# A decoder layer in split float32: buffers of the raw and the low weight parts, and the order of the low products

## The chip, the cores and the metric

The kernel runs on one core of one Trainium2 chip. The metric is the device time of one execution in microseconds (us); lower is better. The core has five engines that each work through a queue of their own, in order: TensorE (PE, with its weight loads shown apart as PEld), VectorE (DVE), ScalarE (ACT), GpSimd (POOL) and SyncE (SP, which here issues the DMAs). [...]

## The reference, cut to what matters

One pre-norm decoder layer over 1024 tokens of width 1024, in float32:

```python
h = rms_norm(x, attn_norm)
z = h @ w_in
a_conv, q, kc_r, vc_r, ks, vs, kw, vw, g = jnp.split(z, splits, axis=-1)
conv_out = conv_mixer(a_conv, ...)              # GLU, causal conv of width 31, LayerNorm, silu
kc = compress(kc_r, cmp_k_pe, cmp_k_w1, cmp_k_w2)
vc = compress(vc_r, cmp_v_pe, cmp_v_w1, cmp_v_w2)
nsa_out = nsa_attention(q, kc, vc, ks, vs, kw, vw, gates)
x = x + concatenate([conv_out, nsa_out]) @ w_out
h = rms_norm(x, ffn_norm)
gate, up = split(h @ w_gate_up)
x = x + (silu(gate) * up) @ w_down
return rms_norm(x, final_norm)
```

The attention has 12 query heads over 4 groups of keys and values and three gated branches: compressed blocks, eight selected blocks, and a window of 512 tokens.

## The kernel before

**Products in split float32.** A product of two float32 matrices is made of three products of parts: each operand is split into a high part (a rounded copy) and a low part (what the copy lacks), and high times high, high times low and low times high are summed in one PSUM bank. The product of the two low parts is left out.

**Weights.** `load_w` (L214) brings one chunk of weights: 128 partitions with up to 1096 numbers each, 512 KB for a chunk of 128 columns. Its steps, in order: one or two DMAs by SP into a raw tile (L224), a cast by ACT into the high tile (L225), and a subtraction by POOL, in four pieces, into the low tile (L229; for the first two chunks it is one piece on DVE). The tile pool `wp` has two raw buffers, three high ones and three low ones. A raw buffer is free again when the low part has been made; a high or low buffer when the last product with it is done. While the first half of the attention runs (`phase[0] == 0`), L220 puts a one-column copy by POOL ahead of the load, which reads a row sum of the attention four steps back (`PACE_B = 4`), so that the load can't start before it.

**Feeds.** A `Feed` (L193) holds a list of such loads. Taking chunk n (`get`) issues the loads up to chunk n+2; a taker that holds two chunks at a time takes the second with `get(1)`, which issues one less.

**Who uses chunks, in order.** Ahead of the attention the feed `first` gives: four chunks for the convolution's input (`conv_in`, each one `gemm_t`: 8 contraction steps with 3 products, 24 products of 512 columns), two for the keys to be compressed (`compress_in`, each used for both halves of the tokens, in the order half 0 with chunks 0 and 1, then half 1 with chunks 0 and 1), two for the window values (`values`, four tiles of tokens in `value_tile`, 24 products of 274 columns each, both chunks in every tile), then four chunks of the compression's first weight in turn with four query chunks (`compress`, 24 products of 264 columns a chunk; `project_d`), two more query chunks, and the same again for the compressed values with four key chunks. Two value chunks at the very start are used tile by tile while the tokens arrive. In all that is chunks 0 to 29.

**The attention** (`attention`, L697) works on 128 queries and one group at a time, first for tokens 0 to 511, then 512 to 1023. `weave` (L175) lays products of a second stream, `fill`, between its products: in the first half `fill_b` (L971), the projections of the second half of the tokens (chunks 30 to 47, by the same helpers), and then, in `fill_all` (L1404), the first output projection (`out_proj`, chunks of `w_out` through another feed) and the feed-forward part. Per step of the attention: products of queries and keys (L788, L792), a fused add with row minimum on DVE (L796), exp on ACT (L799), row sums and their reciprocals on DVE (L803, L804), a scaling on POOL (L809), transposes on PE (L815), the split of the transposed tile by ACT and DVE (L233), and products with the values (L832, L833). `cmp_stage` (L616) makes the compressed branch: products L628, adds on DVE (L630, L632), exp on ACT (L642), scalings on POOL (L646, L650), transposes (L656) and their split (L661, L662), and a store (L663).

**What sets the order.** The program is built with `TileContext(nc, schedule_with_timeline_sim=True)`: a list schedule takes, at each point of a model of the timeline, the first instruction in program order that is ready, and so fixes each engine's queue. On the chip the queues run in that order whatever the real durations are. `Drive` (L149) ties side streams to the matmul that they are emitted behind.

In the functions below the order of the three products is the same everywhere: for each contraction step high with high, then the weights' low part, then the activations' low part:

```python
for a, b in ((wh, hhi), (wl, hhi), (wh, hlo)):
```

Of the kernel before, what the change touches and what calls it, by code (L numbers as in the profile page):

```python
# [12 lines left out]
F32 = mybir.dt.float32  # L13
F32R = mybir.dt.float32r
# [5 lines left out]
P = 128  # L20
# [3 lines left out]
KT = DM // P  # L24
# [24 lines left out]
WCH = 1096  # L49
# [39 lines left out]
def tile_hymba(ctx: ExitStack, tc, x, attn_norm, w_in, conv_w, conv_b, conv_ln_g, conv_ln_b,  # L89
# [10 lines left out]
    wp = ctx.enter_context(tc.tile_pool(name="weights", bufs=3, side="left"))  # L100
# [5 lines left out]
    def bank(name, tag="z"):  # L106
        return ps.tile([P, 512], F32, tag=tag, name=name, bufs=BANKS[tag])
# [27 lines left out]
    MM = 0.216  # L135
# [8 lines left out]
    def mm(*args, **kw):  # L144
        lastpe[0] = pe.matmul(*args, **kw)  # L145
# [62 lines left out]
    def acc_bank(name):  # L208
        turn[0] += 1
        return bank(name, turn[1][turn[0] % len(turn[1])])  # L210

    pace = []

    def load_w(parts, a, b, eng=pool):  # L214
        raw = wp.tile([P, WCH], F32, tag="raw", name="w_raw", bufs=2)
        hi = wp.tile([P, WCH], F32R, tag="whi", name="w_hi")
        lo = wp.tile([P, WCH], F32R, tag="wlo", name="w_lo")
        back = PACE_B if phase[0] == 0 else PACE_C
        if len(pace) >= back > 0:
            pool.tensor_copy(raw[:, 0:1], pace[-back][:, 0:1])  # L220
        n = a * b
        v = raw[:, :n].rearrange("p (k c) -> p k c", k=a)
        for c, src in parts:
            sp.dma_start(v[:, :, c:c + src.shape[-1]], src.rearrange("(k p) c -> p k c", p=P))  # L224
        act.copy(hi[:, :n], raw[:, :n])  # L225
        step = n // PIECES if eng is pool else n
        for c in range(0, n, step):
            q = slice(c, c + step)
            eng.tensor_sub(lo[:, q], raw[:, q], hi[:, q].bitcast(F32))  # L229
        return (hi[:, :n].rearrange("p (k c) -> p k c", k=a), lo[:, :n].rearrange("p (k c) -> p k c", k=a))  # L230

    def split(hi, lo, src):
        return act.copy(hi, src), dve.tensor_sub(lo, src, hi.bitcast(F32))  # L233
# [34 lines left out]
    def quarters(h, w):  # L268
        if h:
            return [pm.tile([P, 4, 512], F32R, tag=("act", "x1")[w], name="h1", bufs=2) for _ in range(2)]  # L270
        return [pa.tile([P, 4, 512], F32R, name=f"h0_{w}_{j}") for j in range(2)]

    hhi = [quarters(h, 0) for h in range(2)]
    hlo = [quarters(h, 1) for h in range(2)]

    def win_chunk(c0):
        return load_w([(0, w_in[0, :, c0:c0 + P])], KT, P)
# [7 lines left out]
    def value_tile(ws, g0, dst, t):  # L285
        hf = t // 4
        o = acc_bank("vo")
        n = 0
        tt = slice((t % 4) * P, (t % 4 + 1) * P)
        for k in range(KT):  # L290
            wh, wl = ws[k // 4]
            for a, b in ((hhi, wh), (hhi, wl), (hlo, wh)):
                mm(o[:, :274], a[hf][k // 4][:, k % 4, tt], b[:, k % 4, :], start=n == 0, stop=n == 3 * KT - 1)
                n += 1
                yield 0.117
        vv = p1.tile([P, GROUPS, 2, HD], F32R, tag="vv", name="vv", bufs=2)
        split(vv[:, :, 0, :], vv[:, :, 1, :], o[:, :256].rearrange("p (g d) -> p g d", g=GROUPS))
        dve.tensor_copy(gates[:, t, g0:g0 + 18], o[:, 256:274])
        sp.dma_start(dst[t * P:(t + 1) * P, :, :], vv.bitcast(F32).rearrange("p g s d -> p g (s d)"))
# [14 lines left out]
    for t in range(6):  # L314
# [7 lines left out]
        if t == 0:  # L322
# [5 lines left out]
            for j, copy in enumerate((dve.tensor_copy, act.copy)):  # L328
                b = bank("gb", "s")
# [87 lines left out]
        pool.tensor_copy(base[:, T + P:], base[:, 512:768])  # L417

    def gemm_t(o, wh, wl, hf):
        n = 0  # L420
        for k in range(KT):
            for a, b in ((wh, hhi), (wl, hhi), (wh, hlo)):
                mm(o, a[:, k, :], b[hf][k // 4][:, k % 4, :], start=n == 0, stop=n == 3 * KT - 1)
                n += 1
                yield MM

    def project_d(feed, dst, row, halves, scaled=False):
        wh, wl = feed.get()
# [37 lines left out]
    def silu(u, th):  # L466
        act.activation(th, u, AF.Tanh)
        dve.scalar_tensor_tensor(u, th, 1.0, u, op0=ALU.add, op1=ALU.mult)

    def compress(xh, xl, feed, w2, tag, out):  # L470
        hs = [bank("h0", tag), bank("h1", tag)]
        n = 0
        for jc in range(4):
            wh, wl = feed.get()
            if jc == 1:
                w2r = pa.tile([P, 2, HD], F32, tag="w2r", name="w2r")
                pool.tensor_copy(w2r[:, 0, 0:1], wh[:, 0, 0:1].bitcast(F32))
            for j4 in range(4):
                j, s = (jc * 4 + j4) % 8, jc // 2
                for a, b in ((wh, xh), (wl, xh), (wh, xl)):  # L480
                    for ht in range(2):
                        mm(hs[ht][:, :264], a[:, j4, ht * P:(ht + 1) * P], b[:, j, :, s:s + 66],
                           start=n < 2, stop=n >= 94)
                        n += 1
                        yield 0.12
        ah = pa.tile([P, 2, 256], F32R, tag="ah", name="ah")
        al = pa.tile([P, 2, 256], F32R, tag="al", name="al")
        for ht in range(2):
            bc = pa.tile([P, 1], F32, tag="bc", name="bc", bufs=2)
            dve.tensor_scalar(bc, hs[ht][:, 64:65], 0.5, None, op0=ALU.mult)  # L490
            af, th = [pa.tile([P, 256], F32, tag="af", name="af", bufs=2) for _ in range(2)]
            dve.tensor_scalar(af.rearrange("p (g n) -> p g n", g=GROUPS),
                              hs[ht][:, :264].rearrange("p (g n) -> p g n", g=GROUPS)[:, :, 0:64],
                              0.5, bc, op0=ALU.mult, op1=ALU.add)
            silu(af, th)
            split(ah[:, ht, :], al[:, ht, :], af)
        sp.dma_start(w2r, w2[0].rearrange("(t p) d -> p t d", p=P))
        w2h = pa.tile([P, 2, P], F32R, tag="w2h", name="w2h")
        w2l = pa.tile([P, 2, P], F32R, tag="w2l", name="w2l")
        for c in range(2):  # L500
            split(w2h[:, :, c * HD:(c + 1) * HD], w2l[:, :, c * HD:(c + 1) * HD], w2r)
        out.extend((ah, al, w2h, w2l))
# [389 lines left out]
    def q_load(m):  # L892
        return lambda: win_chunk(C_Q + m * P)

    def kv_loads():
        return [lambda c=c, m=m: win_chunk(c + m * P) for m in range(2) for c in (C_KW, C_KS)]
# [74 lines left out]
    def fill_b():  # L971
        f1 = Feed([q_load(0), q_load(1)] + value_loads(C_VS, 0) + [q_load(2)] + value_loads(C_VW, 18)
                  + [q_load(m) for m in (3, 4, 5)] + kv_loads() + conv_loads())
        for m in (0, 1):
            yield from project_d(f1, q_d, m * P, (1,), True)
        yield from values(f1, 0, vs_d, 1)
        done.add(("q", 0))
        yield from project_d(f1, q_d, 2 * P, (1,), True)
        done.add(("q", 1))
        yield from values(f1, 18, vw_d, 1)  # L980
        done.update({("v", 0), ("v", 1)})
        for m in (3, 4):
            yield from project_d(f1, q_d, m * P, (1,), True)
        done.add(("q", 2))
        yield from project_d(f1, q_d, 5 * P, (1,), True)
        done.add(("q", 3))
        for dst in (kw_d, ks_d):
            yield from project_d(f1, dst, 0, (1,))
        done.add(("kv", 0))
        for dst in (kw_d, ks_d):  # L990
            yield from project_d(f1, dst, P, (1,))
        done.add(("kv", 1))
        yield from conv_in(f1, 1)
        done.add(("conv", "in"))
# [19 lines left out]
    for (g, qt), at in zip(stages, CMP_AT):  # L1014
        s = cmp_stage(g, qt)
# [47 lines left out]
    def mixed(si, kq):  # L1063
        return ("conv", si) in done and all(("mix", g, i) in done for g in range((2, GROUPS)[kq]) for i in SETS[si])
# [338 lines left out]

    def fill_all():  # L1404
        yield from fill_b()
        while not mixed(0, 0):
            yield -1.0
        mix = mix_in(0, 0, pm)
        set_in(0, pm)
        x_in(0, 0)  # L1410
        x_in(0, 1)
        yield LEAD_C
        yield from out_proj(feed, 0, "z", mix, 0)

        while not mixed(0, 1):
            yield -1.0
        p1_stack.close()
        last["p3"], p = open_pool("p3", "left")
        mix2 = mix_in(0, 1, p, "h21")
        yield from out_proj(feed, 0, "z", mix, 1)  # L1420
        yield MIXLAT
        for ch in range(2):
            yield from out_proj(feed, 0, "z", mix2, ch)
        set_norm(0, p)
        yield from ffn_norm_in(0, "z")
        for _ in range(NF // 2):
            yield from ffn(feed, (0,), FT)
# [87 lines left out]
```

## Time and profile before

| | us |
|---|---|
| three runs | 1472.18, 1472.75, 1474.23 |
| median | 1472.75 |
| profiled execution | 1470.28 |
| its span | 1468.6 |
| its granted TensorE clock | 0.995 |
| PE busy | 1422.3 |
| PEld busy | 1228.5 |
| DVE busy | 1035.2 |
| ACT busy | 771.9 |
| POOL busy | 693.0 |

Times in views are microseconds from the span's start. A row of a timeline gives the start, the duration, the engine, the line, the operation, out<-in with its form, and the count of equal instructions merged; in brackets stands the engine's idle time just before and what ended it. The ends of matmuls are modelled, so that PE appears busy across short pauses; a pause is better seen between the weight loads, as each matmul has one. SPq is the queue of SP, where a row is the issue of a DMA. DMA rows in the chain run from the issue to the landing.

### The profile page before, as it was taken

How to read it: one execution, taken by the hardware profiler on the slowest of the kernel's cores; microseconds unless marked ns; L12 is line 12 of the kernel's file. 1: busy time of each engine (PE TensorE's matmuls, PEld its weight loads, DVE VectorE, ACT ScalarE, POOL GpSimd, SP SyncE). 2: the span in 40 equal slices, each digit the busy share in tenths (PEclk: the TensorE clock that was granted, in tenths of full speed). 3: DMA queues.
4: the chain of work that ended last, by engine and by line, in shares of the span. 5: the costliest groups of instructions: out<-in, count | busy, mean ns of one | idle time of the engine just before them, and what ended most of it. 6: DMA issues, size and time to landing. Idle time of an engine off the chain costs nothing.

```text
span 1468.6 us, 23484 instructions
## 1 busy us (share of the span) xinstructions
PE 1422.3 (97%) x7995; PEld 1228.5 (84%) x7995; DVE 1035.2 (70%) x2279; ACT 771.9 (53%) x1602; POOL 693.0 (47%) x972
## 2 busy tenths in 40 slices
PE   7999999998999999999999999999999999999997
PEld 6888888886878788888888888777887899999996
DVE  5893486778776667687577785512538988788885
ACT  6333466768665566756657564312425544444443
POOL 4666584767665455655655556644568000000001
PEclk9999999999999999999999999999999999999999
DMA  6336578757597244345245213744234433323321
GB/s 218 89 96 187 150 221 243 194 181 214 140 288 218 78 106 121 92 106 132 85 101 137 76 48 98 212 133 150 80 105 155 142 101 107 95 87 115 111 62 72
DMA packets 234246, 196.34 MB, mean 134 GB/s; under 512 B 14745, under 2 KB 204029, under 8 KB 234126
## 3 DMA queue, kind: packets, MB, share of 16 engines
q1 hardware_dynamic: 234126, 194.84, 45.8%
q8 instruction: 63, 1.03, 0.3%
q14 instruction: 57, 0.47, 0.1%
HBM read 161.04 MB, written 33.75 MB: 133 GB/s over the span
## 4 chain that ended last, share of the span: by engine, by line
PE 73%; DVE 10%; DMA 7%; POOL 4%; ACT 3%; issue 2%; SPq 1%; ACTq 0%; POOLq 0%; DVEq 0%
PE gu L1154 17%; PE dn L1173 14%; PE yy L1301 7%; PE pt L815 5%; PE zo L145 4%; PE zz L1301 3%; PE wo L1088 3%; DMA w_raw<-in_w_in_dram 3%; PE s L788 3%; PE o L833 3%; PE o L832 3%; DVE cacc L571 2%; POOL w_lo L229 2%; PE vo L145 2%; DMA o_raw<-in_w_out_dram 2%
## 5 line engine op out<-in xcount | busy, mean ns | idle before, releaser
L229 POOL TENSOR_TENSOR w_lo<-w_raw,w_hi 128x256 fp32r<-128x256 f32 (+1 forms) x504 | 406.0, 837 | 161.0 <-ACT w_hi L225 154.1
L1154 PE MATMUL gu<-h,w_hi 128*128 128x512 f32 x768 | 253.0, 398 | 0.6 <-DVE x L1178 0.6
L1173 PE MATMUL dn<-w_hi,aw 128*128 128x512 f32 x656 | 230.7, 397 | 1.6 <-DVE x L1178 1.2
L225 ACT CAST w_hi<-w_raw 128x1024 fp32r<-128x1024 f32 (+1 forms) x147 | 152.7, 1051 | 130.6 <-DMA w_raw<-in_w_in_dram 43.1
L809 POOL TENSOR_SCALAR pr<-pr,l,gates 128x640 f32<-128x640 f32 (+5 forms) x192 | 148.4, 785 | 122.4 <-DVE l L804 96.0
L233 DVE TENSOR_TENSOR pl<-pt,ph 128x384 fp32r<-128x384 f32 x264 | 140.4, 551 | 54.8 <-ACT ph L233 52.8
L799 ACT ACTIVATE pr<-pr,m 128x640 f32<-128x640 f32 (+5 forms) x192 | 141.5, 737 | 71.0 <-DVE m L796 69.2
L1154 PEld LDWEIGHTS gu<-h,w_hi 128*128 128x128 f32 x768 | 143.2, 188 | 29.5 <-DVE x L1178 1.0
L233 ACT CAST ph<-pt 128x384 fp32r<-128x384 f32 x264 | 118.9, 478 | 81.2 <-PE pt L815 61.6
L1383 POOL TENSOR_TENSOR rs<-rs,mhalf 128x1 f32<-128x1 f32 x4 | 2.6, 643 | 319.1 <-DVE rs L1382 318.9
L1154 PE MATMUL gu<-h,w_lo 128*128 128x512 f32 x384 | 152.3, 397 | 0.0
L1173 PEld LDWEIGHTS dn<-w_hi,aw 128*128 128x128 f32 x656 | 123.2, 188 | 27.5 <-DVE x L1178 2.1
L1178 DVE TENSOR_TENSOR x<-dn,x 128x512 f32<-128x512 f32 x168 | 113.4, 685 | 42.2 <-PE dn L1173 41.5
L815 PE MATMUL pt<-ident,pr 128*128 128x128 f32 x792 | 136.8, 273 | 5.0 <-DVE pl L233 3.7
L1173 PE MATMUL dn<-w_lo,aw 128*128 128x512 f32 x328 | 129.6, 395 | 0.0
L796 DVE CUSTOM_DVE_ANT_0 pr<-s,base 128x384 f32<-128x384 f32 (+3 forms) x192 | 101.2, 533 | 33.2 <-PE s L792 19.8
L815 PEld LDWEIGHTS pt<-ident,pr 128*128 128x128 f32 x792 | 101.4, 140 | 22.5 <-issue 3.2
L145 PE MATMUL zo<-h,w_hi 128*128 128x512 f32 x320 | 106.9, 402 | 2.0 <-ACT w_hi L225 1.2
L1247 ACT CAST w_s<-sum 128x512 fp32r<-128x512 f32 x80 | 49.3, 621 | 106.8 <-PE yy L1301 89.5
L788 PE MATMUL s<-kt,q 128*128 128x384 f32 (+3 forms) x288 | 100.8, 352 | 4.3 <-DVE m L796 1.8
L832 PE MATMUL o<-ph,vt 128*128 128x384 f32 x264 | 98.7, 374 | 2.3 <-ACT ph L233 1.3
L1301 PEld LDWEIGHTS yy<-term,w_s 128*128 128x128 f32 x720 | 93.1, 188 | 8.4 <-DVE c L1316 3.5
(271 smaller groups left out, 3163.7 us busy)
## 6 DMA issues: line engine op xcount, KB each, us to landing
w_raw<-in_w_gate_up_dram SPq DMA_DIRECT2D x48, 512.0 KB, 3.9
w_raw<-in_w_down_dram SPq DMA_DIRECT2D x43, 512.0 KB, 3.6
w_raw<-in_w_in_dram SPq DMA_DIRECT2D x40, 512.0 KB, 4.3
u_raw<-in_w_gate_up_dram SPq DMA_DIRECT2D x20, 512.0 KB, 5.0
g_raw<-in_w_gate_up_dram SPq DMA_DIRECT2D x19, 512.0 KB, 3.9
qc<-q_d SPq DMA_DIRECT2D x32, 192.0 KB, 3.9
pc_d<-pct SPq DMA_DIRECT2D x16, 384.0 KB, 4.1
pct<-pc_d SPq DMA_DIRECT2D x32, 192.0 KB, 4.4
```

The lines of the kernel that those rows point to most:

```text
L145: lastpe[0] = pe.matmul(*args, **kw)
L225: act.copy(hi[:, :n], raw[:, :n])
L229: eng.tensor_sub(lo[:, q], raw[:, q], hi[:, q].bitcast(F32))
L233: return act.copy(hi, src), dve.tensor_sub(lo, src, hi.bitcast(F32))
L788: pe.matmul(sv, q2[0], kk_[:, 0, kk], start=True, stop=False)
L799: act.activation(pr[:, :n], pr[:, :n], AF.Exp, bias=m, scale=-1.0, accum_out=l3[:, r:r + 1])
L809: pool.tensor_scalar(x_, x_, l3[:, r2:r2 + 1], gates[:, i, c:c + 1], op0=ALU.mult, op1=ALU.mult)
L815: pe.transpose(pt[:, r * P:(r + 1) * P], prs[st][1 + r][:, kk * P:(kk + 1) * P], ident)
L832: pe.matmul(o[:, :384], v, ph, start=False, stop=False)
L1154: pe.matmul(o, w[:, k, :], h2[si][h][k // 4][:, k % 4, :], start=n == 0, stop=n == 3 * KT - 1)
L1173: pe.matmul(o, aws[si][:, a, k, t * P:(t + 1) * P], b[:, 0, ch * 512:(ch + 1) * 512], start=n == 0, stop=n == 5)
L1301: pe.matmul(o, w[:, k, :], h[:, k, :], start=fresh and n == 0, stop=n == 11, skip_group_check=not fresh)
```

## The change

`wp` keeps eight weight buffers of one size: the third low buffer becomes a buffer with the tag `swing`. Until `fill_b` has been emitted, raw chunks rotate over three buffers (two of their own and the swing one) and low parts over two; after that it is two and three as before, when the first output projection's loads are emitted. The high parts keep three buffers. In `value_tile`, `gemm_t` and `compress`, all products with the high weights come first and those with the low weights last; in each fourth tile of `value_tile` it is the other way round, the low ones first. `out_proj` and everything behind it keep their order. The number of products and loads is unchanged.

```diff
+    swing, turns = ["raw"], {"raw": 0, "wlo": 0}
+
+    def w_tile(kind, dt, name):
+        turns[kind] += 1
+        if swing[0] == kind and turns[kind] % 3 == 0:
+            return wp.tile([P, WCH], dt, tag="swing", name=name, bufs=1)
+        return wp.tile([P, WCH], dt, tag=kind, name=name, bufs=2)
+
     def load_w(parts, a, b, eng=pool):
-        raw = wp.tile([P, WCH], F32, tag="raw", name="w_raw", bufs=2)
+        raw = w_tile("raw", F32, "w_raw")
         hi = wp.tile([P, WCH], F32R, tag="whi", name="w_hi")
-        lo = wp.tile([P, WCH], F32R, tag="wlo", name="w_lo")
+        lo = w_tile("wlo", F32R, "w_lo")
...
-        for k in range(KT):
-            wh, wl = ws[k // 4]
-            for a, b in ((hhi, wh), (hhi, wl), (hlo, wh)):
-                mm(o[:, :274], a[hf][k // 4][:, k % 4, tt], b[:, k % 4, :], start=n == 0, stop=n == 3 * KT - 1)
-                n += 1
-                yield 0.117
+        his = [(a, k, 0) for k in range(KT) for a in (hhi, hlo)]
+        los = [(hhi, k, 1) for k in range(KT)]
+        order = los + his if t % 4 == 3 else his + los
+        for n, (a, k, w) in enumerate(order):
+            mm(o[:, :274], a[hf][k // 4][:, k % 4, tt], ws[k // 4][w][:, k % 4, :], start=n == 0, stop=n == 3 * KT - 1)
+            yield 0.117
...
     def gemm_t(o, wh, wl, hf):
-        n = 0
-        for k in range(KT):
-            for a, b in ((wh, hhi), (wl, hhi), (wh, hlo)):
-                mm(o, a[:, k, :], b[hf][k // 4][:, k % 4, :], start=n == 0, stop=n == 3 * KT - 1)
-                n += 1
-                yield MM
+        order = [(wh, b, k) for k in range(KT) for b in (hhi, hlo)] + [(wl, hhi, k) for k in range(KT)]
+        for n, (a, b, k) in enumerate(order):
+            mm(o, a[:, k, :], b[hf][k // 4][:, k % 4, :], start=n == 0, stop=n == 3 * KT - 1)
+            yield MM
...
-            for j4 in range(4):
+            for a, b, j4 in [(wh, b, j4) for j4 in range(4) for b in (xh, xl)] + [(wl, xh, j4) for j4 in range(4)]:
                 j, s = (jc * 4 + j4) % 8, jc // 2
-                for a, b in ((wh, xh), (wl, xh), (wh, xl)):
-                    for ht in range(2):
-                        mm(hs[ht][:, :264], a[:, j4, ht * P:(ht + 1) * P], b[:, j, :, s:s + 66],
-                           start=n < 2, stop=n >= 94)
-                        n += 1
-                        yield 0.12
+                for ht in range(2):
+                    mm(hs[ht][:, :264], a[:, j4, ht * P:(ht + 1) * P], b[:, j, :, s:s + 66],
+                       start=n < 2, stop=n >= 94)
+                    n += 1
+                    yield 0.12
...
     def fill_all():
         yield from fill_b()
+        swing[0] = "wlo"
         while not mixed(0, 0):
```

More of the change, by code (lines that the diff above doesn't have):

```diff
@@ L419, in gemm_t @@
     def gemm_t(o, wh, wl, hf):
-        n = 0
-        for k in range(KT):
-            for a, b in ((wh, hhi), (wl, hhi), (wh, hlo)):
-                mm(o, a[:, k, :], b[hf][k // 4][:, k % 4, :], start=n == 0, stop=n == 3 * KT - 1)
-                n += 1
-                yield MM
+        order = [(wh, b, k) for k in range(KT) for b in (hhi, hlo)] + [(wl, hhi, k) for k in range(KT)]
+        for n, (a, b, k) in enumerate(order):
+            mm(o, a[:, k, :], b[hf][k // 4][:, k % 4, :], start=n == 0, stop=n == 3 * KT - 1)
+            yield MM
     def project_d(feed, dst, row, halves, scaled=False):
```

## The prediction

> **What bounds the kernel now.** I read the page first, then the windows table over the stretches in which the edited helpers run, then the waits of the weight loads there.
>
> ```profile
> PE 1422.3 (97%) x7995; PEld 1228.5 (84%) x7995; DVE 1035.2 (70%) x2279; ACT 771.9 (53%) x1602; POOL 693.0 (47%) x972
> ```
> ```profile
> 20.00:100.00 80.00, 77.39 (x438) 67.80 (x437) 69.28 (x114) 31.45 (x60) 46.19 (x51) 0.98 0.32 100
> 100.00:240.00 140.00, 135.30 (x751) 116.13 (x750) 84.38 (x200) 68.25 (x194) 94.94 (x133) 1.00 0.68 198
> 240.00:420.00 180.00, 169.68 (x973) 143.89 (x972) 136.81 (x458) 127.23 (x378) 117.75 (x189) 0.99 0.67 186
> ```
>
> The columns are the stretch, its length, busy time and count of PE, PEld, DVE, ACT, POOL, the granted clock, the DMA share and GB/s. PE is the bound in all three: its idle time is 2.6, 4.7 and 10.3 us. The edited helpers end near 420 us, so 17.6 us of PE idle time is the whole stake, of which only waits for weights can go. The matmul rate itself doesn't change: one projection's 24 products of 512 columns start as follows.
>
> ```profile
> 168.02 0.40 PE L145 MATMUL zo<-h,w_hi 128*128 128x512 f32 x1
> 173.37 0.62 PE L145 MATMUL zo<-h,w_hi 128*128 128x512 f32 x2
> ```
>
> The last row's first product is the 24th, so 23 steps take 5.35 us, 0.233 each, high and low weights alike; a chunk takes 24 x 0.233 = 5.58 us in any order of its products.
>
> The waits for weights, from the timeline of the weight loads, with one wait that hangs on ACT:
>
> ```profile
> 130.60 0.19 PEld L145 LDWEIGHTS zo<-h,w_hi 128*128 128x128 f32 x1 [0.53 <-ACT w_hi L225]
> 131.41 0.19 PEld L145 LDWEIGHTS zo<-h,w_lo 128*128 128x128 f32 x1 [0.62 <-POOL w_lo L229]
> 137.84 0.19 PEld L509 LDWEIGHTS kc<-ah,w2h 128*128 128x128 f32 x1 [0.69 <-ACT ah L233]
> 204.74 0.19 PEld L145 LDWEIGHTS zo<-h,w_hi 128*128 128x128 f32 x1 [1.40 <-ACT w_hi L225]
> 205.55 0.19 PEld L145 LDWEIGHTS zo<-h,w_lo 128*128 128x128 f32 x1 [0.62 <-POOL w_lo L229]
> 259.56 0.30 PEld L145 LDWEIGHTS vo<-w_hi,h 128*128 128x128 f32 x2 [0.93 <-ACT w_hi L225]
> 407.92 0.19 PEld L145 LDWEIGHTS cv<-h,w_hi 128*128 128x128 f32 x1 [1.06 <-ACT w_hi L225]
> 408.73 0.19 PEld L145 LDWEIGHTS cv<-h,w_lo 128*128 128x128 f32 x1 [0.63 <-POOL w_lo L229]
> ```
>
> **The third raw buffer, ahead of the attention.** With two raw buffers a load starts when the low part two chunks back is made. One turn, from the chain and the engines' timelines:
>
> ```profile
> 187.89 2.79 POOL L229 TENSOR_TENSOR w_lo<-w_raw,w_hi 128x256 fp32r<-128x256 f32 x4
> 194.93 2.82 POOL L229 TENSOR_TENSOR w_lo<-w_raw,w_hi 128x256 fp32r<-128x256 f32 x4 [0.30 <-ACT w_hi L225]
> 198.99 4.58 DMA w_raw<-in_w_in_dram
> 203.65 1.04 ACT L225 CAST w_hi<-w_raw 128x1024 fp32r<-128x1024 f32 x1 [0.25 <-DMA w_raw<-in_w_in_dram]
> SPq L224 <- POOL w_lo L229: 63.3, 26, 5.7
> ```
>
> The low part that ends at 197.75 frees the buffer; the load is issued 1.24 us later, lands after 4.58, and the cast ends at 204.69, just ahead of PE's row at 204.74. The last line (waits of SP's queue up to 240 us) says that this is the rule: 26 issues stood 63.3 us for it. With three raw buffers this load waits for the low part before, which ended at 187.89 + 2.79 = 190.68, so it may start 7.1 us sooner. The cast then waits for a high buffer (three as before, free when the chunk three back is done) and no longer for a landing. So the high waits at 130.60 and 204.74 go: 0.53 + 1.40. SP, freed sooner, issues what stands behind its load sooner; the added early loads at the very start follow six loads of tokens in program order, so they don't delay these.
>
> [...]
>
> ACT's queue has work behind such casts:
>
> ```profile
> 129.50 1.05 ACT L225 CAST w_hi<-w_raw 128x1024 fp32r<-128x1024 f32 x1 [5.28 <-DMA w_raw<-in_w_in_dram]
> 132.68 1.05 ACT L225 CAST w_hi<-w_raw 128x1024 fp32r<-128x1024 f32 x1 [2.13 <-DMA w_raw<-in_w_in_dram]
> 133.64 0.41 ACT L467 ACTIVATE af<-af 128x256 f32<-128x256 f32 x1
> 125.10 0.48 DVE L492 TENSOR_SCALAR af<-h,bc 128x256 f32<-128x256 f32 x1
> ```
>
> The tanh of the compression has its input at 125.58 and starts at 133.64, behind two casts that wait for DMAs. What it feeds is the product at 137.84; with earlier landings that 0.69 goes too.
>
> **Low products last.** A chunk's low part is then wanted 16 products, 16 x 0.233 = 3.7 us, after its first product. The three low waits (0.62, 0.62, 0.63) end 0.8 us after the first product, so all three go.
>
> Sum removed: 0.53 + 0.62 + 0.69 + 1.40 + 0.62 + 0.63 = 4.49, less six normal pauses between two loads (0.233 - 0.19 = 0.04 each): **4.25 us**.
>
> **Two low buffers: what is added.** POOL's subtraction for chunk n+2 now waits until PE is done with chunk n; behind it in POOL's queue stand the scalings of the compressed branch and of the attention. Its price is 2.79 us in the rows above, and at most:
>
> ```profile
> 76.24 5.65 POOL L229 TENSOR_TENSOR w_lo<-w_raw,w_hi 128x274 fp32r<-128x274 f32 x4 [8.50 <-ACT w_hi L225]
> ```
>
> In the plain case it may start as chunk n ends and is wanted 5.58 + 3.7 = 9.3 us later: 3.6 us to spare even at 5.65. After a compression chunk and a query chunk it is about 7.5. The tight place is the boundary from `compress_in` to the window values. The second value chunk's low buffer comes free only with the last key product, and PE wants it after 20 of the 274-column products:
>
> ```profile
> 78.91 0.29 PE L145 MATMUL vo<-w_hi,h 128*128 128x274 f32 x1
> 88.31 0.28 PE L145 MATMUL vo<-w_hi,h 128*128 128x274 f32 x1
> 90.35 0.51 PE L145 MATMUL h<-xh,w_hi 128*128 128x264 f32 x2 [1.76 <-ACT xh L233]
> 91.90 0.36 PE L145 MATMUL vo<-w_hi,h 128*128 128x274 f32 x1 [0.78 <-DVE gates L298]
> ```
>
> 72 products of three tiles and one of the fourth lie from 78.91 to 88.31, 0.13 each; the last of the four pieces is wanted after 23 x 0.13 = 3.0 us and made after 2.79 to 5.65: a new wait of 0 to 2.7 us. I put it at nothing, since PE stands 1.76 + 0.78 us soon after for DVE, whatever it did before; without that cover it costs up to 2.7. For the other places I let one low wait like the three that go come back: 0.58.
>
> **Low parts in the attention's first half.** Here the third raw buffer is worth nothing, and I count no gain from it:
>
> ```profile
> 224.78 2.98 POOL L229 TENSOR_TENSOR w_lo<-w_raw,w_hi 128x274 fp32r<-128x274 f32 x4 [1.40 <-DMA mix_d<-m]
> 253.36 0.30 POOL L220 COPY w_raw<-l 128x1 f32<-128x1 f32 x2
> 253.98 1.13 SPq L224 DMA_DIRECT2D w_raw<-in_w_in_dram  x2
> ```
>
> The raw buffer had been free since 227.8, and the load went with the pacing copy at 253.36, so the high waits at 259.56 and 407.92 stay. Most paced loads come late enough that their low buffer is free already. Three low parts do move: the query chunk behind the first values (230.09 before), the one behind the second (276.67), and the second chunk of `w_out` (416.11).
>
> **Sum.** 4.25 - 0.58 = 3.67 us off. The profiled execution took 1470.28 (span 1468.6, and 1.68 around it), so 1466.6 by it; it lies 2.47 under the median of 1472.75, and from the median the forecast is **1469.1**.
>
> **The rivals.** *The stage chains gain as well.* The tanh that was 8 us late starts a chain (compression, compressed scores, transposes) on which PE waits later:
>
> ```profile
> 187.98 0.55 PE L656 MATMUL pt<-ident,pg 128*128 128x128 f32 x3 [0.50 <-POOL pg L650]
> 189.26 0.47 PE L145 MATMUL zo<-h,w_hi 128*128 128x512 f32 x1 [0.73 <-DVE pct L662]
> PEld s L788 <- DVE m L796: 4.6, 10, 1.3
> ```
>
> If these two go (1.2) and the attention's waits for the row minima, 4.6 us in ten stands, fall by half (2.3), it is 3.5 more: 1465.6. For it: ACT stood tens of us at casts here. Against it: the ten stands are the attention's own, away from these helpers.
>
> *The gain is absorbed at the entry to the attention.* There the DMA engines are full:
>
> ```profile
> 220.00:240.00 20.00, 18.93 (x128) 17.40 (x128) 13.70 (x42) 12.68 (x42) 11.23 (x17) 1.00 1.00 291
> ```
>
> If the first keys and values land no sooner, what was won before 240 us is waited away, and only 408.73's 0.59 stays: 1472.2. Against it: PE still is busy 18.93 of 20 there, with fill work at hand, and earlier weight loads leave this stretch emptier.
>
> *Slower: POOL's queue in the attention.* The three moved low parts fall into the attention's own POOL work.
>
> ```profile
> 230.09 2.99 POOL L229 TENSOR_TENSOR w_lo<-w_raw,w_hi 128x256 fp32r<-128x256 f32 x4 [2.33 <-ACT w_hi L225]
> 276.67 2.84 POOL L229 TENSOR_TENSOR w_lo<-w_raw,w_hi 128x256 fp32r<-128x256 f32 x4 [1.33 <-ACT w_hi L225]
> 286.05 1.30 POOL L809 TENSOR_SCALAR pr<-pr,l,gates 128x128 f32<-128x128 f32 x3
> 287.30 0.30 POOL L220 COPY w_raw<-l 128x1 f32<-128x1 f32 x2
> 416.11 2.83 POOL L229 TENSOR_TENSOR w_lo<-w_raw,w_hi 128x256 fp32r<-128x256 f32 x4 [0.95 <-PE ut L687]
> ```
>
> The one at 276.67 would start after about 282, ahead of the scalings at 286.05 and of the pacing copy, which lets the next loads go. Each such group costs up to its length, 2.99 + 2.84 + 2.83 = 8.7, if PE has no fill products meanwhile; against 4.25 that is 4.4 slower: 1477.2. One of them uncovered turns the forecast into no change, all three decide it. For it: POOL is 65% busy from 240 to 420. Against: before the first one POOL has long idle times. [...]
>
> *The change doesn't do what it says*: the building lays out all queues anew by its model, and may move other work where a buffer is late in the model. No row prices this; it spreads each case by a few us, and the range holds it.
>
> **How the numbers follow.** A measurement of this kernel can tell about 0.2%, 2.95 us, from no change. Forecast 0.45, four fifths of it beyond that bound; chains gain too 0.15; absorbed 0.22; slower 0.18. Faster: 0.36 + 0.15 = 0.51; same: 0.09 + 0.22 = 0.31; slower 0.18. The range goes from 1463, under the second case, to 1476.5, which leaves out the end of the last.
>
> **What would show it.** Right: no PE wait for `w_hi` near 130 and 204; none for a low part; SP's waits for POOL's low parts far under 63 us; POOL's idle time before a low part ended by PE rather than by ACT; the start of attention some 3.5 us earlier and the same distance kept to the end. Wrong: PE waits for `w_lo` at a boundary of values, for `pr` of L809 after 280, or the attention starting no earlier.

## The result, and the profile after

The changed kernel takes 1488.6 us (median of 6 runs, 1483.91 to 1491.04) beside 1472.89 (6 runs, 1471.28 to 1474.23): a ratio of 1.0099, 95% interval 1.0086 to 1.0112. It is 15.7 us slower where 3.7 us less were forecast, and above the range. Its profiled execution took 1491.04, span 1489.3. First the engines' line of the page, then the same three stretches as before, with the same columns.

```profile
PE 1431.7 (96%) x7995; PEld 1239.5 (83%) x7995; DVE 1027.0 (69%) x2279; ACT 771.3 (52%) x1602; POOL 691.1 (46%) x972
```
```profile
20.00:100.00 80.00, 75.70 (x420) 66.29 (x419) 67.27 (x111) 30.79 (x60) 43.62 (x49) 0.96 0.33 94
100.00:240.00 140.00, 133.04 (x699) 114.23 (x698) 76.63 (x178) 62.59 (x170) 91.24 (x127) 0.95 0.61 176
240.00:420.00 180.00, 167.53 (x971) 145.70 (x971) 131.93 (x463) 123.58 (x378) 113.17 (x183) 0.97 0.68 188
```

PE's idle time rises from 2.6, 4.7 and 10.3 us to 4.3, 7.0 and 12.5, and the granted clock falls from 0.98, 1.00 and 0.99 to 0.96, 0.95 and 0.97. Between 100 and 240 us PE gets 699 matmuls done, against 751. Finer stretches (length, PE busy, clock, DMA share, GB/s), with the sums over the execution, show where; first before, then after:

```profile
0.00:100.00 100.00, 88.50 (x482) 0.98 0.43 134
100.00:180.00 80.00, 79.11 (x391) 1.00 0.55 160
180.00:260.00 80.00, 73.89 (x461) 1.00 0.81 238
260.00:420.00 160.00, 151.98 (x874) 0.99 0.66 183
420.00:560.00 140.00, 134.64 (x731) 0.99 0.59 164
...
sum 1500.00, PE 1422.26; mean PE 203.18
```
```profile
0.00:100.00 100.00, 86.85 (x468) 0.97 0.44 131
100.00:180.00 80.00, 80.00 (x403) 1.00 0.57 165
180.00:260.00 80.00, 70.59 (x422) 0.91 0.73 214
260.00:420.00 160.00, 149.99 (x848) 0.97 0.65 176
420.00:560.00 140.00, 130.33 (x690) 0.96 0.62 169
...
sum 1500.00, PE 1431.67; mean PE 204.52
```

Matmuls differ in size, so their counts show only roughly how far the work has come. From 100 to 180 us the change does what the prediction says: PE has no pause left, with 403 matmuls instead of 391. But this only makes good 12 of the 14 that the first 100 us had lost. Then 39 are lost in 80 us, 26 in the next 160 and 41 in the 140 behind them: by 560 us 108 in all, of which the stretch looked at below is the first part. Over the whole span the same 7995 matmuls take 1431.67 - 1422.26 = 9.4 us longer, and PE stands idle 1489.3 - 1431.67 = 57.6 us instead of 1468.6 - 1422.26 = 46.3, 11.3 more; together that is the 20.7 us between the spans. The waits of the weight loads from 20 to 560 us (in total, times, longest):

```profile
PEld wo L1092 <- DMA mix<-mix_d: 5.0, 3, 2.4
...
PEld sc L632 <- issue: 4.1, 1, 4.1
...
PEld zo L145 <- ACT pct L665: 3.2, 1, 3.2
```

None of the long ones is for a low part. The last two stand before these PE rows; behind them the ten-microsecond stretches around them, of after and then of before (columns as at the top):

```profile
194.48 1.51 PE L632 MATMUL sc<-kc,qc 128*128 128x128 f32 x6 [3.88 <-DMA qc<-q_d]
...
211.81 3.75 PE L145 MATMUL zo<-h,w_hi 128*128 128x512 f32 x8 [2.98 <-DVE af L496]
```
```profile
190.00:200.00 10.00, 6.04 (x27) 5.85 (x28) 5.58 (x18) 3.14 (x13) 6.48 (x11) 0.68 0.77 216
...
210.00:220.00 10.00, 8.19 (x27) 6.69 (x28) 6.20 (x21) 5.39 (x19) 3.22 (x5) 0.66 0.79 235
```
```profile
190.00:200.00 10.00, 10.00 (x64) 9.04 (x63) 7.12 (x19) 6.09 (x18) 7.12 (x10) 1.00 0.84 271
200.00:210.00 10.00, 8.49 (x49) 7.02 (x48) 8.39 (x27) 6.53 (x21) 8.35 (x12) 1.00 0.81 229
```

The pause of 3.88 us is paid twice: the clock falls with it to 0.68 in its ten microseconds, and only 27 matmuls are done in that stretch, against 64 (of other sizes) before.

In stretches of two microseconds the clock of the changed kernel is 0.90 from 192 to 194 us, 0.50 from 194 to 200 and 1.00 from 202 to 204. Around the pause of 2.98 us, which ends at 211.81, it is 0.66 from 210 to 212, 0.50 from 212 to 216 and 1.00 from 218 to 220.

Why does PE stand at 194.48? (The wait at 211.81 was not traced further.) In the kernel before, the scores `sc` came behind the 24 products of the third key projection (kv2, 189.26 to 194.90), and found their queries landed:

```profile
187.81 0.58 SPq L620 DMA_DIRECT2D qc<-q_d  x1
```
```profile
194.90 0.78 PE L628 MATMUL sc<-kc,qc 128*128 128x128 f32 x6
```

In the changed kernel SP issues this load at 189.58, but PE has the scores ahead of kv2 in its queue:

```profile
189.58 0.58 SPq L624 DMA_DIRECT2D qc<-q_d  x1
```

In the program's text kv2 stands ahead of these scores in both kernels. The scheduler moved it. Comparing the queues of the two built programs, place by place, 2705 of PE's 7993 places hold another instruction than before, and 257 or more of each other engine's; the last changed place of PE is its 3694th. Behind it nothing more is lost: the 3701st matmul in order of time starts at 701.05 us before and at 722.05 after, 21.0 us later, and the spans differ by 20.7. So the change has two effects: its own, and another order of the work around it.

### The profile page after: what moved, and what is told of

It is laid out like the page before. It is cut to its first block, busy times and chain, and to the rows that moved or that the text cites. A ratio compares the mean times of both kernels' runs of the same rounds, so it can differ in the third digit from the quotient of the medians.

```text
span 1489.3 us, 23487 instructions
## 1 busy us (share of the span) xinstructions
PE 1431.7 (96%) x7995; PEld 1239.5 (83%) x7995; DVE 1027.0 (69%) x2279; ACT 771.3 (52%) x1602; POOL 691.1 (46%) x972
## 4 chain that ended last, share of the span: by engine, by line
PE 73%; DVE 10%; DMA 9%; POOL 3%; ACT 3%; issue 2%; SPq 0%; ACTq 0%; POOLq 0%; DVEq 0%
PE gu L1158 16%; PE dn L1177 14%; PE yy L1305 7%; PE zo L145 5%; PE pt L819 5%; PE zz L1305 3%; PE wo L1092 3%; PE o L837 3%; PE o L836 2%; PE s L792 2%; DVE cacc L575 2%; DMA w_raw<-in_w_in_dram 2%; DMA o_raw<-in_w_out_dram 2%; PE aa L1305 2%; PE vo L145 2%
## 5 line engine op out<-in xcount | busy, mean ns | idle before, releaser
L813 POOL TENSOR_SCALAR pr<-pr,l,gates 128x640 f32<-128x640 f32 (+5 forms) x192 | 149.1, 789 | 132.7 <-DVE l L808 109.2
L1305 PE MATMUL yy<-term,w_s 128*128 128x256 f32 x720 | 95.1, 281 | 3.5 <-DVE c L1320 3.5
```

What stands on the lines that cost most here:

```text
L813: pool.tensor_scalar(x_, x_, l3[:, r2:r2 + 1], gates[:, i, c:c + 1], op0=ALU.mult, op1=ALU.mult)
L1305: pe.matmul(o, w[:, k, :], h[:, k, :], start=fresh and n == 0, stop=n == 11, skip_group_check=not fresh)
```

## The experiments

Each ratio is to the kernel before on the same chip, with its 95% interval; no experiment has the number 4. "Places" are those of PE's 7993 that hold another instruction than in the kernel before, counted in the built programs.

| experiment | places | us | ratio | interval |
|---|---|---|---|---|
| the change | 2705 | 1488.6 | 1.0099 | 1.0086 to 1.0112 |
| 1 order alone | 2704 | 1494.4 | 1.0133 | 1.0111 to 1.0156 |
| 2 buffers alone | 4833 | 1485.0 | 1.0069 | 1.0050 to 1.0088 |
| 3 swing back early | 4649 | 1502.3 | 1.0188 | 1.0162 to 1.0214 |
| 5 order alone, queues held | 0 | 1476.4 | 1.0027 | 1.0001 to 1.0053 |
| 6 the change, queues held | 0 | 1478.6 | 1.0037 | 1.0020 to 1.0054 |
| 7 before, PE as after | 2705 | 1500.6 | 1.0187 | 1.0155 to 1.0220 |
| 8 swap of two products | 4343 | 1494.2 | 1.0145 | 1.0104 to 1.0185 |
| 9 the change, PE held | 0 | 1478.2 | 1.0029 | 1.0015 to 1.0042 |
| 10 swap, queues held | 0 | 1471.7 | 0.9989 | 0.9974 to 1.0004 |
| 11 as 5, old value tiles | 0 | 1474.7 | 1.0014 | 0.9998 to 1.0029 |
| 12 as 6, old value tiles | 0 | 1476.5 | 1.0023 | 1.0006 to 1.0040 |
| 13 one edge | 3967 | 1491.5 | 1.0118 | 1.0098 to 1.0137 |
| 14 swap in value tiles | 184 | 1474.0 | 1.0004 | 0.9990 to 1.0019 |

**The halves of the change (1 to 3).** Experiment 1 keeps the changed order of products, with two raw and three low buffers as before. Experiment 2 keeps the changed buffers, with the old order. Experiment 3 is the change with the swing buffer given back to the low parts earlier, as the attention begins.

```diff
     def w_tile(kind, dt, name):
         turns[kind] += 1
-        if swing[0] == kind and turns[kind] % 3 == 0:
-            return wp.tile([P, WCH], dt, tag="swing", name=name, bufs=1)
-        return wp.tile([P, WCH], dt, tag=kind, name=name, bufs=2)
+        return wp.tile([P, WCH], dt, tag=kind, name=name, bufs=2 if kind == "raw" else 3)
```
```diff
+    swing[0] = "wlo"
     pc_stack, pc = open_pool("pc", "right")
...
     def fill_all():
         yield from fill_b()
-        swing[0] = "wlo"
```

The first diff is that of experiment 1, the second that of 3, both against the changed kernel; experiment 2 is the kernel before with the `w_tile` and `swing` lines of the change alone. Two theories stood at the start: A, that two low buffers cost the time, since low parts are made just in time; B, that the low products' place at the end costs it.

> Only the order of the products is changed; raw chunks keep two buffers and low parts three. Theory A (the two low buffers cost the time: POOL's subtractions become just in time and hold up what is queued behind them): about the time of before, 1470 to 1475 us, with the PE waits for low parts near 131, 205 and 408 us gone. Theory B (the low products at the end cost it: PSUM banks and the low buffers are held in another order, so that all queues are laid out worse): most of the 15.7 us lost stays, 1483 to 1490.

> Only the buffers are changed (three raw, two low up to the first output projection); the products keep the order of before, so that PE wants a chunk's low part with its second product. Theory A: slower than the changed kernel, 1495 to 1520 us, since each low part is now wanted 3.7 us sooner. Theory B: near before, 1470 to 1478.

> The changed kernel, but the third buffer goes back to the low parts when the attention's second stream begins to be emitted (ahead of chunk 30), instead of after it. By the landmarks in the trace the changed kernel has lost 11.5 us by the end of the first values of the second stream (255.0 against 243.6) and 14.3 by the end of the last convolution chunk (431.9 against 417.6). Theory A in its first form (low parts in the attention hold up POOL there): 1474 to 1479, only the loss before 240 us stays. If the loss is made between 186 and 215 us, before the attention: 1483 to 1489, hardly better.

Each half costs by itself (1.33% and 0.69%), the whole costs less than the first half alone (0.99%), and the variant that should lighten the load on two low buffers is the dearest. So neither theory holds, and the effects don't add. That led to theory C: what costs is the order that the scheduler lays out anew, whichever edit sets it off.

**Queues held (5, 6, 7, 9).** Each of these kernels carries in `ORDER` (kept packed) the places of an engine's instructions as another kernel has them, and adds an edge without a semaphore from each instruction to the next of its engine; no instruction is added. The lines that unpack `ORDER` are left out below. Since both kernels issue the same instructions from the same places of the text, a place of one is a place of the other.

```diff
+def pin(tc, nc):
+    ins = list(nc.cur_bb.bb.instructions)
+    why = mybir.DependencyInfo(mybir.DependencyClass.NoSync, mybir.DependencyReason.DATA)
+    for queue in ORDER.values():
+        for i, j in zip(queue, queue[1:]):
+            tc.add_manual_dep(ins[j], ins[i].name, why, reason="pinned order")
...
     with _tile.TileContext(nc, schedule_with_timeline_sim=True) as tc:
         tile_hymba(tc, *args)
+        pin(tc, nc)
```

Experiment 5 holds all five engines of experiment 1's kernel, 6 all but GpSimd in the changed kernel, 9 PE alone in the changed kernel; 7 gives PE of the kernel before the order of the changed one.

> The order-only kernel (products with a low part last, raw two and low three buffers, 1494.4 us, +19 over before), with one thing added: a list at its end gives each of the five engines the same order of its instructions as in the kernel before, instruction for instruction (each product stands for the product of the same place in its group). No instruction is added or taken away. Theory C (the scheduler laid 2704 of PE's 7993 places, and 235 to 793 of the other engines', in another order, and that new order costs the 19 us): back to before or a little under it, 0.997 to 1.002 of it. Theory B (the products' own order costs it, whatever the queues): about 1.010 to 1.014.

> The changed kernel whole (three raw and two low buffers, low products last), with PE, VectorE, ScalarE and SyncE held to the order that they have in the kernel before; GpSimd's queue is left to the scheduler, since its low parts must wait for two low buffers. Theory C: the wait at 194 us (sc for qc) and the one at 211 go and the time is that of before or up to 4 us under it, 0.997 to 1.003. Theory A (two low buffers, the low parts made just in time): still 1.005 to 1.011 slower, with PE waiting for w_lo. Theory B: 1.010.

> The kernel before, its buffers and its products' order within a group unchanged, with PE alone held to the order of the changed kernel; the other four queues are laid out to go with it. Theory C: the loss comes with the order, 1.004 to 1.012 slower, with a wait of sc for qc or its like near 190 us. Theories A and B: nothing that they blame is there, 0.998 to 1.002.

> The changed kernel with PE alone held to the order that it has in the kernel before; the other four queues are laid out to go with it (129 of SyncE's 638 places, 168 to 225 of the others' differ from before). Theory C, if it is PE's order that lost the cover at 194 and 211 us: most of the 15.7 us comes back, 1.000 to 1.006. If the order of SyncE's transfers and of the casts does it as well, it stays between, 1.006 to 1.010.

With the queues held, experiment 1's 1.33% falls to 0.27% and the change's 0.99% to 0.37%, with PE held alone to 0.29%. In the other direction the kernel before, given the changed kernel's order on PE, is 1.87% slower without any of the change's edits, and more than the change itself is; its other four queues were laid out a third way. Both 6 and 7 lie above what theory C forecast for them (0.997 to 1.003 and 1.004 to 1.012): the order isn't the whole loss, and one engine's order doesn't fix its size. The waits of experiment 7 from 20 to 560 us have the scores among them, at 194.07 us, as forecast:

```profile
...
PEld sc L628 <- issue: 2.9, 1, 2.9
```

**A swap that is nothing by itself (8, 10, 14).** Experiment 8 is the kernel before with one edit in `gemm_t`; 10 is the same with all five queues held; 14 is the like edit in `value_tile`.

```diff
-            for a, b in ((wh, hhi), (wl, hhi), (wh, hlo)):
+            for a, b in ((wh, hhi), (wh, hlo), (wl, hhi)):
                 mm(o, a[:, k, :], b[hf][k // 4][:, k % 4, :], start=n == 0, stop=n == 3 * KT - 1)
```

> The kernel before with one edit: in each k step of the transposed projections the second and third of the three products change places (low part of the weight times high part of the rows comes third). Buffers are those of before, and each k step still uses all three, so what a chunk holds, and for how long, moves by one product of some 0.23 us. The scheduler gives 4343 of PE's places to other instructions for it. Theory C: the time moves by more than 0.3 per cent, likelier up (1.004 to 1.015). Theories A and B: 0.999 to 1.001.

> The kernel before with the second and third product of each k step of the transposed projections changing places (its own queues cost 1.0145), now with all five queues in the order of before. Theory C: 0.998 to 1.002, so that the swap itself is worth nothing and its 21 us are the layout's. Otherwise it stays above 1.008.

> The kernel before with the second and third of the three products of each k step of the value tiles changing places (a like edit to the swap that cost 1.0145). This time the scheduler moves only 184 of PE's 7993 places and 6 to 72 of the other engines', none of PE's beyond its 1436th. Theory C: little is re-laid, so little is lost: 0.998 to 1.004. If the swap of products itself were what costs, it would be 1.005 or more, as the value tiles have 384 such products against the 480 of the projections.

The swap costs 1.45% when the scheduler lays 4343 places anew, and nothing when it may not (0.9989, interval 0.9974 to 1.0004). Its twin moves 184 places and costs nothing that can be measured. In the profile of experiment 8 the longest waits are for rows of the attention, high parts and the rows to be compressed (20 to 560 us):

```profile
PEld wo L1088 <- DMA mix<-mix_d: 7.0, 5, 1.9
PEld zo L145 <- ACT w_hi L225: 5.0, 5, 2.6
PEld h L145 <- ACT xh L233: 4.1, 1, 4.1
```

Much of the loss stands where no product was swapped. The helpers with the edit end near 420 us, yet the 5041st matmul in order of time starts at 970.86 us instead of 962.88 and the 5601st at 1112.27 instead of 1090.69: 13.6 us are lost between them. The rows are of before, of experiment 8 (columns as in the finer stretches), and of the longest wait in experiment 8 there, for high parts of the weights of a later output projection. In the kernel before the waits for these come to 1.2 us.

```profile
960.00:1120.00 160.00, 158.31 (x697) 1.00 0.36 111
```
```profile
960.00:1120.00 160.00, 151.17 (x634) 0.96 0.33 101
```
```profile
PEld wo L1109 <- ACT o_hi L1035: 6.5, 3, 4.4
```

This is the cleanest of the tests: same buffers, same products, only the order of the queues differs between 8 and 10.

**One cover put back (13).** The changed kernel with one edge, which lays the scores of 194.48 us behind kv2 again.

```diff
         tile_hymba(tc, *args)
+        ins = list(nc.cur_bb.bb.instructions)
...
+        tc.add_manual_dep(ins[1632], ins[1617].name, why, reason="scores behind kv2")
```

> The changed kernel, its queues left to the scheduler but for one edge: the compressed scores that stood at 194.48 us (sc, waiting 3.9 us for qc) come behind the last of the 24 products of the kv2 projection, as they do in the kernel before. The edge makes the scheduler give 3593 of PE's places to other instructions than in the changed kernel. If the loss were that one lost cover and the clock that fell with it: 1480 to 1483 us, some 6 to 9 less than the changed kernel's 1488.6. Theory C, that the loss is of the whole re-laid stretch: the wait at 194 us goes, but other waits come, and the time is anywhere from 1478 to 1500.

It is no faster than the change. The wait didn't go, it moved to a later set of scores and grew:

```profile
208.41 1.51 PE L632 MATMUL sc<-kc,qc 128*128 128x128 f32 x6 [6.37 <-DMA qc<-q_d]
```

One edge made the scheduler lay thousands of places anew, and a like wait turned up elsewhere. So mending the one place didn't mend the loss. What that place alone is worth this run doesn't show, and theory C's range for it, 1478 to 1500, was too wide to be much of a test.

**What the change does on held queues (11, 12).** Both put the value tiles back to the old order of products, 12 all but each fourth one.

```diff
-        order = los + his if t % 4 == 3 else his + los
+        order = los + his if t % 4 == 3 else [(a, k, w) for k in range(KT) for a, w in ((hhi, 0), (hhi, 1), (hlo, 0))]
```

> The order-only kernel on the queues of before (raw two, low three buffers; 1.0027 with its value tiles changed too), with the value tiles put back to the products' order of before; low parts come last in the transposed projections and in the compression alone. Theory D (with high parts first a value tile runs through all eight k steps in 16 of its 24 products, so the first ones wait for VectorE's rows: 1.75 us of it before 20 us, against 0.2): about 1.5 us less than the kernel with all three, 0.998 to 1.002. The three low waits at 131.41, 205.55 and 408.73 should be gone (1.87 us).

> The changed kernel with PE, VectorE, ScalarE and SyncE in the order of before (1.0037), with the first three value tiles of each half put back to the products' order of before; the fourth keeps its low parts first, which two low buffers need. Theory D: the waits for rows before 20 us go, 1.000 to 1.002; the gain that was forecast at 130.60, 131.41, 137.84, 204.74 and 205.55 (4 us of the forecast 4.25) stays, so 0.997 if nothing else gives it back. Otherwise 1.002 to 1.005.

The waits that theory D names are there. From 0 to 100 us, first before, then experiment 5:

```profile
PEld vo L145 <- DVE h L233: 0.2, 1, 0.2
```
```profile
PEld vo L145 <- DVE h L239: 1.7, 3, 0.7
```

But the gains against 5 and 6 (0.0013 and 0.0014 of the ratio) lie within the intervals, so theory D isn't settled by the times. No version beat the kernel before.

## Why the prediction was wrong, point by point

**The step that failed** is the last rival: "the building lays out all queues anew by its model, and may move other work where a buffer is late in the model. No row prices this; it spreads each case by a few us". The mechanism was named, and its size was wrong. The changed kernel pays about 1.0029 to 1.0037 with PE's order held and 1.0099 without, so the new order is some two thirds of the loss, 9 to 10 us, where "a few us" stood. In other variants it is more: seven kernels whose queues were laid anew over thousands of places are 0.7 to 1.9% slower, 10 to 28 us. The loss doesn't go with the number of places (4833 for 0.69%, 2705 for 0.99%). The range of 13.5 us left no room for it. That a changed queue could lose a cover such as kv2, and the clock with it (0.68 from 190 to 200 us, 1.00 before), was nowhere in my sum.

That term is only half of the miss, which is 15.7 + 3.7 = 19.4 us. The rest lies in the sum itself: with PE's order held the change is 0.29 to 0.37% slower, 4 to 5.5 us, and not 3.7 us faster. The points below say which terms failed. An order made for the old buffers may also hold the new ones back; these runs can't part that from the change.

**The waits up to 180 us went**, as said: those at 130.60, 131.41 and 137.84, for 1.84 us in all. From 100 to 180 PE is busy 80.00 of 80.00. But the attention didn't start sooner for it: its first product of queries and keys starts at 233.72 us before, at 242.49 in the changed kernel and at 233.83 in experiment 12.

**The wait at 204.74 did not go** on held queues, and here the step itself was wrong: "this load waits for the low part before, which ended at ... 190.68, so it may start 7.1 us sooner". In experiment 12, with three raw buffers, SP issues this load at 198.85, 0.14 us sooner than the 198.99 of before. From the timelines of SP, ACT and PEld in experiment 12:

```profile
196.17 1.49 SPq L446 DMA_DIRECT2D kw_d<-zh  x1
197.75 0.38 SPq L446 DMA_DIRECT2D kw_d<-zl  x1
198.18 0.58 SPq L624 DMA_DIRECT2D qc<-q_d  x1
198.85 0.57 SPq L232 DMA_DIRECT2D w_raw<-in_w_in_dram  x1
```
```profile
203.95 1.04 ACT L233 CAST w_hi<-w_raw 128x1024 fp32r<-128x1024 f32 x1 [1.73 <-DMA w_raw<-in_w_in_dram]
```
```profile
205.04 6.73 PEld L145 LDWEIGHTS zo<-h,w_hi 128*128 128x128 f32 x23 [1.49 <-ACT w_hi L233]
```

The load stands in SP's queue behind the stores of the keys just projected and a load of queries, which wait for their own producers: from 186 to 204 us these stores stand 1.8 us in two waits and the loads of queries 3.8 in four, beside 0.4 for a low part. The buffer was one of two causes; I had priced the one that came last and not looked for the next, although the prediction's own waits of SP were the place to look. The low wait at 205.55 is gone: the 23 loads of the last row follow one another without a wait, some of them at a lower clock (0.83 from 200 to 210 us, see the last section).

SP's waits for POOL's low parts were to fall far under 63 us up to 240. They didn't: they are 72.2 us in the changed kernel and 49.0 in experiment 6. From SP's waits and POOL's timeline of the changed kernel:

```profile
SPq L232 <- POOL w_lo L237: 72.2, 22, 18.4
```
```profile
94.66 6.20 POOL L237 TENSOR_TENSOR w_lo<-w_raw,w_hi 128x256 fp32r<-128x256 f32 x6 [10.94 <-PE vo L145]
```

POOL's idle time is now ended by PE, as said, and that takes back the third raw buffer: a raw buffer is held until its low part is made, and the low part waits for a low buffer. With three and two, as with two and three, load n waits for the products of chunk n-5. That follows from the buffers, and I had overlooked it when I let the load depend on one low part alone.

**The boundary to the window values** was bounded by 0 to 2.7 us and put at nothing. In the timeline of PEld from 78 us on, first before, then experiment 12:

```profile
81.94 0.19 PEld L145 LDWEIGHTS vo<-w_lo,h 128*128 128x128 f32 x1 [0.30 <-POOL w_lo L229]
90.35 0.30 PEld L145 LDWEIGHTS h<-xh,w_hi 128*128 128x128 f32 x2 [1.98 <-ACT xh L233]
91.87 0.19 PEld L145 LDWEIGHTS vo<-w_hi,h 128*128 128x128 f32 x1 [0.98 <-issue]
```
```profile
81.98 0.19 PEld L145 LDWEIGHTS vo<-w_lo,h 128*128 128x128 f32 x1 [0.71 <-POOL w_lo L237]
83.21 0.19 PEld L145 LDWEIGHTS vo<-w_lo,h 128*128 128x128 f32 x1 [0.81 <-POOL w_lo L237]
84.38 0.19 PEld L145 LDWEIGHTS vo<-w_lo,h 128*128 128x128 f32 x1 [0.75 <-POOL w_lo L237]
91.11 0.30 PEld L145 LDWEIGHTS h<-xh,w_hi 128*128 128x128 f32 x2 [0.34 <-ACT xh L241]
93.03 0.30 PEld L145 LDWEIGHTS h<-xl,w_hi 128*128 128x128 f32 x2 [1.62 <-DVE xl L241]
```

The low waits grow from 0.30 to 2.27 us, those behind them shrink from 2.96 to 1.96. So here the 2 us more of low waits lie within the bound, and the cover hid half: some 1 us is lost. (In experiment 12 the first three value tiles have the old order of products, so the low parts are wanted sooner than the prediction assumed; in experiment 6, with the new order, the low waits up to 100 us come to 1.9 us.) In the changed kernel with its own queues no low part is waited for here, but the two waits behind grow to 3.35 + 1.44 us, the clock from 90 to 100 us is 0.66 beside 0.83 before, and this is where the 14 matmuls of the first 100 us go.

**POOL's queue** was the slower rival. One row of it shows, where PE alone is held (experiment 9), at the place where the kernel before waited 0.50 us for the same scaling:

```profile
191.44 0.34 PEld L660 LDWEIGHTS pt<-ident,pg 128*128 128x128 f32 x3 [4.56 <-POOL pg L654]
```

It lies ahead of the attention, not in it, and the waits for the scalings of the attention, L813, don't grow in the changed kernel: 1.1 us in four up to 560 us, beside 2.3 before (3.1 in seven in experiment 6). The rival's sign was right, its place wrong.

**The absorbed rival** holds on held queues, but at another entry. In experiment 9 PE comes to the first output projection early and waits for the attention's rows; PE rows of before, then of experiment 9:

```profile
418.91 0.47 PE L1088 MATMUL wo<-w_hi,mix 128*128 128x512 f32 x1 [0.58 <-DMA mix<-mix_d]
```
```profile
420.10 0.77 PE L1092 MATMUL wo<-w_hi,mix 128*128 128x512 f32 x1 [6.78 <-DMA mix<-mix_d]
```

PE was there at 420.10 - 6.78 = 413.3 instead of 418.91 - 0.58 = 418.3, 5 us sooner than before, and started 1.2 us later. What PE had gained ahead of this point the attention took back. The other profiles of the change with PE's order held lose time in the same stretch. The rows are of before and of experiment 12 (columns as in the finer stretches):

```profile
380.00:490.00 110.00, 103.83 (x565) 0.98 0.73 212
```
```profile
380.00:490.00 110.00, 99.79 (x541) 0.97 0.74 213
```

By 490 us experiments 6, 9 and 12 have done 2530, 2538 and 2535 matmuls. The kernel before has done 2551, and so has experiment 10, the swap on held queues. Up to 380 us the three were not behind (1987, 2008 and 1994, against 1986). In experiment 12 the longest waits there are for high parts (4.3 us), for the attention's values (3.3) and for its rows (2.1). Even with the order held the change is therefore no gain; of its 0.2 to 0.4% this stretch is the largest part seen, the boundary above another. Why these transfers come late there is not shown, and each figure is from one profile.

**What stays open.** Why the order before is the better one. The runs show that each of seven others laid out anew in the large is worse, not what in the scheduler's model makes it choose them, nor whether an order exists that lets the change gain. With two low buffers GpSimd can't be held to the old order (a low part would stand ahead of work which the products that free its buffer wait for), so the change on fully held queues wasn't tried.

## What to carry to other kernels

Where a list scheduler fixes the queues, compare the queues before comparing the times: count the places that changed, and hold the old order by edges to part what an edit does from what its new order does. A wait that is removed is worth only what the next cause leaves, so list what stands ahead in the issuing queue as well as the buffer. And a single pause of 2.98 us on TensorE cost more than its length here, since the clock went down with it (0.50 from 212 to 216 us): the next eight products took 3.75 us, against 8 x 0.233 = 1.86. So look for the work that covers a DMA which is just in time. To put one cover back by an edge, with the rest left to the scheduler, gained nothing (experiment 13).

## What the runs showed of the hardware that was not expected

Half of the loss between the profiles (9.4 of 20.7 us) is no idle time: the same products keep PE busy longer, at a granted clock of 0.984 over the changed kernel's span, 0.995 before. After the pause of 2.98 us, too, the next products of 512 columns take 3.75 / 8 = 0.47 us each, against 0.233, while the pause of 1.40 us at 204.74 in the kernel before left its ten microseconds (200 to 210) at a clock of 1.00. A pause of nearly that length went otherwise: in experiment 12 PE stands 1.49 us at the same place, after 0.57 us at 203.14, and there the clock is 0.83. What parts the two is not shown.

```profile
200.00:210.00 10.00, 8.32 (x43) 6.91 (x42) 7.12 (x20) 6.12 (x20) 7.27 (x10) 0.83 0.85 229
```

The changed kernel's runs also lie further apart, 1483.91 to 1491.04 against 1471.28 to 1474.23; why was not tested.
